# Small transfers of a decoder block issued by POOL and ScalarE instead of SyncE

## The chip, the cores and the metric

The kernel runs on one core of one Trainium2 chip, in one launch. The metric is the device time of one execution in microseconds (us). Four engines compute: TensorE (PE, with its weight loads shown apart as PEld), VectorE (DVE), ScalarE (ACT) and GpSimd (POOL). SyncE (SP) computes nothing here; it only issues transfers (DMAs). Every engine works through its own instructions strictly in order, and an instruction that waits for a semaphore holds up all that stands behind it on that engine. An engine that issues a DMA spends some time on the issue itself; the bytes are then moved by 16 DMA engines that all issuers share.

## What is computed

One post-norm decoder block on a sequence of 16 meta tokens and 1024 input rows of width 1024, in float32. A combined projection feeds two mixers that run side by side: a grouped state-space model (S5: 32 groups of 16 channels, 64 complex states each) and a chunkwise matrix LSTM with four heads. Their gated sum goes through an output projection, a layer norm and a feed-forward network of width 4096. Cut to what matters:

```python
h = _layer_norm(concat([meta, x]), ln0_g, ln0_b)                 # 1040 rows
p = h @ w_in + b_in          # columns: u_s5 | q | k | v | o | i | f | g_s5 | g_m
y_s5 = _s5_mixer(u_s5, ...)  # x_t = Abar x_{t-1} + Bbar u_t ; y_t = Re(C x_t) + D u_t, per group
z = gelu(y_s5) @ s5_w_glu
y_s5 = z[..., :D] * sigmoid(z[..., D:])
q, k = split(silu(causal_depthwise_conv(concat([q, k]))))        # width 4
hm = _mlstm_mixer(q, k, v, i, f)                                 # 4 heads, chunkwise, with a running maximum
y_m = (sigmoid(o) * head_norm(hm)) @ m_w_out
mix = sigmoid(g_s5) * y_s5 + sigmoid(g_m) * y_m
h = _layer_norm(ALPHA * h + mix @ w_o, ln1_g, ln1_b)
ff = square(relu(h @ w_up + b_up)) @ w_down
out = _layer_norm(ALPHA * h + ff, ln2_g, ln2_b)[16:]
```

## The kernel before

Every float32 matrix product is made of three passes of a cheaper float32 form: each operand is split into a high part (rounded, by ACT: `whi`, L212) and a low part (the rest, by DVE: `wlo`, L213), and `mm3` (L226 to L228) adds high x high, low x high and high x low into one PSUM tile. In the trace the three passes of a projection read `mm<-hT_hi,whi` (L226), `mm<-hT_lo,whi` (L227) and `mm<-hT_hi,wlo` (L228).

The projection is cut into jobs, one per 128 output columns (or per head for the values v), in the order of a string `ORDER` (`q0 q1 v0 q2 v1 q3 o1 o0 v2 ... u0 u1 v3 u2 g0 u3 g1 ...`); glu, gate and output jobs follow, then the feed-forward part. A job's raw weights (`wraw`) are loaded by SP, and split while the job before it runs. Between the matmuls of a job the kernel calls `pump`, which advances six lanes of side work, each a generator that yields an estimate of how long to wait until its next step: the mLSTM heads (`ml`), the convolution (`cv`), the constants of the state-space model (`s5c`), its batches (`s5`), its GELU (`s5g`), and a lane `ah` that scales rows kept for the residual and prepares weights of the feed-forward part. A scheduler then fixes one order of instructions for each engine, by its own estimates of what each costs; it inserts the semaphores too. Almost all working tiles are slots of one pool of 30 buffers (tag `s`), so a load into a slot waits for whoever used that slot last.

The lanes that the change touches, with the names that the traces and orders use:

- **mLSTM, per head:** `bvt` is a broadcast bias (L319). The gates write two small rows to device memory, `grow_dr` (L410) and `wrow_dr` (L413). `bcast_row` (L425, L427) reads a head's part of each back, broadcast over 128 partitions, into `gB` and `wiB`. DVE turns `gB` into a mask (L443); ACT takes its exponential (L446, L447) and scales the keys `kw` with it (L459). `hraw` is a head's raw output; DVE normalises it (L505), PE transposes it (`pt`, L512). `hm_dr` (L892) keeps the finished heads.
- **State space, four batches of 8 groups:** `s5_pre` loads constants (L582 to L588). For each batch the constants lane (`s5c`) builds the matrices `s5P`, `s5Rr`, `s5Ri` (L695 to L718) and, through PE's `s5k` (L739, L740, which need `s5Ri`), the kernel `s5Kt` (L744). Then 16 transfers (L757) spread `s5Kt` into the triangular matrix `s5Mx`. POOL writes the seeds of a table of rotations `s5T` (L763 to L766) and DVE doubles it eight times, six operations a time (L571 to L576, in `cmul`).
- **A batch itself** (`s5_batch`): 8 transfers (L785) gather the inputs `s5U` from `us_dr`, which the projection job u wrote (L545). PE makes `s5z` (L801) from `s5U`; ACT and DVE copy it out (L811, L809); DVE multiplies by the table (L816 to L819), adds (L821, L822), scans (L827), multiplies back (L837 to L840) and adds (L845). PE makes `s5y` from `s5Mx` and `s5U` (L856) and from the scan's result `s5w` (L857). The output goes out to `ys_dr` (L862), comes back rearranged in 8 transfers as `s5yc` (L870), and ACT takes the GELU (L873), which the glu jobs need.
- **Rows and prepared weights** (`ah_scale`, `up_early`): eight tiles of normalised rows are read (`ahr`, L1163), scaled and shifted by DVE and written back (`ah_dr`, L1174). Six weight tiles `wur` (L1190) become 21 prepared tiles that are stored (`wu_dr`, L1200) and read again much later as `wpre` (L1411).

All of these transfers stand on SP, among the weight loads; only the 21 loads `wpre` are issued by POOL.

Of the kernel before, what the change touches and what calls it, by code (L numbers as in the profile page):

```python
# [14 lines left out]
P = 128  # L15
# [97 lines left out]
def decoder_block(  # L113
# [24 lines left out]
    def f32(ap):  # L138
        return ap.bitcast(F32)
# [170 lines left out]
    def v_job(h):  # L310
# [6 lines left out]
        def run(job):  # L317
            bvt = mid.tile([P, DV], F32, tag="bvt", bufs=1, name="bvt")
            nc.sync.dma_start(bvt, row_bcast(bv, DV, h * DV))  # L319
            if h == 0:  # L320
# [43 lines left out]
    def gates():  # L364
        with ExitStack() as gc:
# [43 lines left out]
            v_.tensor_tensor_scan(gg, one, a, mp, op0=OP.add, op1=OP.max)  # L409
            nc.sync.dma_start(grow_dr, gg)  # L410
            wi = gt("lf2")
            a_.activation(wi, gg, AF.Exp, scale=-1.0, bias=mp)
            nc.sync.dma_start(wrow_dr, wi)  # L413
            em = gt("fr2")
# [9 lines left out]
    def bcast_row(dst, src, h):  # L424
        nc.sync.dma_start(dst[:, 0:META], bass.AP(tensor=src.tensor, offset=src.offset + h * P,  # L425
                                                  ap=[[0, P], [1, META]]))
        nc.sync.dma_start(dst[:, META:LEN].rearrange("p (c s) -> p c s", s=P),  # L427
                          bass.AP(tensor=src.tensor, offset=src.offset + (4 + h) * P,
                                  ap=[[0, P], [4 * P, NCH - 1], [1, P]]))
# [104 lines left out]
    def u_job(i):  # L534
        st = {}

        def evac(bi, c0, c1, ps):
            if bi == 0:
                st["u"] = slot("uT")
            o = st["u"][:, :LEN].rearrange("p (j c) -> p c j", j=8)  # L540
            a_.activation(o[:, c0 // 8:c1 // 8, :], ps.rearrange("p (c j) -> p c j", j=8), AF.Identity,
                          bias=bft[:, JU + i:JU + i + 1])

        def done():
            nc.sync.dma_start(us_dr[i * P:(i + 1) * P].rearrange("p j c -> p (j c)"), st["u"][:, :LEN])  # L545
            UD.add(i)
            lanes["s5c"].add(s5_consts(i))
            lanes["s5"].add(s5_batch(i))
        fm_job(JU + i, BLK, 0, evac, done)
# [28 lines left out]
    def s5_pre():  # L578
        def t16(name):
            return mid.tile([P, 16], F32, name="s5_" + name)  # L580
        lam = mid.tile([P, 112], F32, tag="row", bufs=1, name="s5_lam")[:, :48].rearrange("p (a b) -> p a b", a=3)
        nc.sync.dma_start(lam, s5l)  # L582
        bc = slot("s5bc")
        nc.sync.dma_start(bc[:, 0:512], s5b)
        nc.sync.dma_start(bc[:, 512:1024], s5c)
        S5["bc"] = bc
        dtl = mid.tile([32, 16], F32, name="s5_d")
        nc.sync.dma_start(dtl, s5d)  # L588
        S5["d"] = dtl
# [83 lines left out]
    def s5_consts(b):  # L673
# [81 lines left out]
        for j in range(8):  # L755
            for g2 in range(2):
                nc.sync.dma_start(mx[16 * j:16 * j + 16, :, g2, 16 * j:P],  # L757
                                  kt[16 * g2:16 * g2 + 16, :, 0:P - 16 * j])
# [21 lines left out]
    def u_load(b):  # L780
        U = slot("s5U")
        uv = U[:, :8 * NB].rearrange("p (g c) -> p g c", g=8)
        for j in range(8):
            src = us_dr[b * P:(b + 1) * P, j, :].rearrange("(g h) c -> h g c", h=16)
            nc.sync.dma_start(uv[16 * j:16 * j + 16], src)  # L785
        S5["u", b] = U
        return U

    def s5_batch(b):
# [60 lines left out]
        for hf in range(2):  # L850
# [10 lines left out]
            yield Y5[b]  # L861
        nc.sync.dma_start(ys_dr[b].rearrange("p g c -> p (g c)"), Y[:, 0:1024])  # L862
        lanes["s5g"].add(s5_gelu(b))

    def s5_gelu(b):
        yield 3.0
        yc = slot("s5yc")
        for g in range(8):
            src = ys_dr[b, :, (g % 2) * 4 + g // 2, :].rearrange("(t h) c -> h t c", h=16)
            nc.sync.dma_start(yc[16 * g:16 * g + 16, 0:1024].rearrange("p (t c) -> p t c", t=8), src)  # L870
        yield 14.0
# [12 lines left out]
    def o_job(f):  # L884
        def evac(bi, c0, c1, ps):
            if bi == 0:
                o_job.s = slot("osig")
            a_.activation(o_job.s[:, c0:c1], ps, AF.Sigmoid, bias=bft[:, JO + f:JO + f + 1])
            v_.tensor_tensor(HM[f][:, c0:c1], HM[f][:, c0:c1], o_job.s[:, c0:c1], op=OP.mult)

        def done():
            nc.sync.dma_start(hm_dr[f], HM.pop(f)[:, :D])  # L892
        fm_job(JO + f, HALF, META, evac, done)
# [261 lines left out]
    def ah_scale():  # L1155
        gb = [slot("gB0"), slot("bB0")]
        for i in range(2):
            nc.sync.dma_start(gb[i][:, :D], row_bcast(ln0r, D, i * D))
        rs = {}
        for t in range(9):  # L1160
            if t < 8:
                rs[t] = slot("ahr")
                nc.sync.dma_start(rs[t][:, :D], ah0_dr[t * P:(t + 1) * P, :])  # L1163
            if t == 0:
# [6 lines left out]
            for i, op in enumerate((OP.mult, OP.add)):  # L1171
                v_.tensor_tensor(r[:, :D], r[:, :D], gb[i][:, :D], op=op)
                yield 1.5
            nc.sync.dma_start(ah_dr[(t - 1) * P:t * P, :], r[:, :D])  # L1174

# [10 lines left out]
    def up_early():  # L1186
        for p in range(PRE):
            r = [slot("wur"), slot("wur")]
            for j in range(2):
                nc.sync.dma_start(r[j][:, :D], wup[2 * p + j].rearrange("p k f -> p (k f)"))  # L1190
            yield 3.0
# [3 lines left out]
            for n, w in ((1, a11), (2, a12), (3, n2[:, 0:512]), (4, a22), (5, n1[:, 0:512]), (6, n1[:, 512:1024]),  # L1195
# [3 lines left out]
                v_.tensor_tensor(o[:, 512:1024], w, f32(o[:, 0:512]), op=OP.subtract)  # L1199
                nc.sync.dma_start(wu_dr[p, n - 1], f32(o[:, 0:1024]))  # L1200
                yield 0.9
# [666 lines left out]
```

## Time and profile before

| | us |
|---|---|
| median of three executions | 1559.34 (1558.19 to 1671.65) |
| the profiled execution | 1557.0 |
| its span in the trace | 1555.2 |
| PE busy | 1525.8 (98%) |
| DVE busy | 1013.5 (65%) |
| ACT busy | 613.9 (39%) |
| POOL busy | 28.4 (2%) |

The span runs from the first to the last instruction that the trace holds; 1.8 us of the profiled execution lie around it. SP computes nothing and has no busy time on the page; its issues can be read in a timeline or by tile, where it is written SPq. In rows by line or tile, `x` is a number of instructions, and three numbers with slashes are the shortest, median and longest duration in ns. In a table of windows each engine has its busy time in that stretch, and `PEclk`, the third number from the end, is the clock granted to TensorE (1.00 is full speed). A row of waits reads: engine, tile and line that waited, `<-` what ended the wait, then us in total, times, and the longest.

### The profile page before, as it was taken

Reading aid. Unit: us, or ns where it says so; the run is one execution under the profiler, and the core shown is the slowest. Engines: PE = TensorE matmul, PEld = TensorE weight load, DVE = VectorE, ACT = ScalarE, POOL = GpSimd, SP = SyncE. Lnnn points to the kernel's source line nnn. Section 1 sums busy time; section 2 is a strip of 40 time slices with the busy share of each in tenths; the row PEclk is TensorE's granted clock in tenths of the full one; section 3 lists DMA queues with packets and bytes.
Section 4 is the critical chain, followed back from the end, with each engine's and each line's share of the span. In section 5 each row is a group of like instructions: output and inputs, shape, how many; then the busy total and the mean of one; then the engine's idle time right before and its main releaser. Section 6 shows DMA issues by size and latency. Waiting matters only on the chain.

```text
span 1555.2 us, 20386 instructions
## 1 busy us (share of the span) xinstructions
PE 1525.8 (98%) x7677; PEld 1287.7 (83%) x7677; DVE 1013.5 (65%) x2007; ACT 613.9 (39%) x950; POOL 28.4 (2%) x99
## 2 busy tenths in 40 slices
PE   8999999998999999999999999999999999999997
PEld 8999998997878778878888887888888888888886
DVE  7676565678668655742228576666666689766786
ACT  6533434335454333331115334444444534433340
POOL 0000000000000000000000001000000000000000
PEclk9999999999999999999999999999999999999999
DMA  6302113304222566731114328544443897767642
GB/s 249 111 19 79 63 42 99 96 22 114 84 77 65 160 245 228 266 140 41 55 59 174 107 79 263 199 149 149 150 149 122 274 390 269 241 220 240 217 170 103
DMA packets 105058, 232.53 MB, mean 150 GB/s; under 512 B 15912, under 2 KB 33776, under 8 KB 104960
## 3 DMA queue, kind: packets, MB, share of 16 engines
q1 hardware_dynamic: 101936, 220.22, 41.2%
q0 software_dynamic: 3024, 11.01, 2.2%
q8 instruction: 60, 0.98, 0.3%
q14 instruction: 38, 0.31, 0.1%
HBM read 164.41 MB, written 65.61 MB: 148 GB/s over the span
## 4 chain that ended last, share of the span: by engine, by line
PE 76%; issue 16%; DVE 3%; ACT 2%; DMA 2%; SPq 1%; POOLq 0%; DVEq 0%; ACTq 0%
PE mm L226 20%; PE mm L228 20%; PE mm L227 20%; PE sd L227 2%; PE sd L226 2%; PE sd L228 2%; PE mm L1091 2%; DMA wiB<-wrow_dr 1%; PE mm L1099 1%; PE pu L476 1%; PE pn L472 1%; PE pn L473 1%; SPq L757 1%; PE ln L1050 0%; PE s5z L801 0%
## 5 line engine op out<-in xcount | busy, mean ns | idle before, releaser
L226 PE MATMUL mm<-hT_hi,whi 128*128 128x512 f32 (+3 forms) x576 | 217.8, 378 | 1.4 <-ACT whi L212 1.4
L227 PE MATMUL mm<-hT_lo,whi 128*128 128x512 f32 (+3 forms) x576 | 215.6, 374 | 0.0
L228 PE MATMUL mm<-hT_hi,wlo 128*128 128x512 f32 (+3 forms) x576 | 214.9, 376 | 0.0
L213 DVE TENSOR_TENSOR wlo<-wraw,whi 128x1024 fp32r<-128x1024 f32 (+1 forms) x60 | 73.1, 1222 | 81.0 <-ACT whi L212 80.2
L226 PEld LDWEIGHTS mm<-hT_hi,whi 128*128 128x128 f32 x576 | 108.5, 188 | 18.1 <-ACT whi L212 1.8
L227 PEld LDWEIGHTS mm<-hT_lo,whi 128*128 128x128 f32 x576 | 108.5, 188 | 16.8 <-issue 0.4
L228 PEld LDWEIGHTS mm<-hT_hi,wlo 128*128 128x128 f32 x576 | 108.2, 188 | 16.6 <-issue 0.3
L212 ACT ACTIVATE whi<-wraw 128x1024 fp32r<-128x1024 f32 (+1 forms) x60 | 63.0, 1055 | 80.7 <-PE mm L227 74.1
L227 PE MATMUL sd<-dwl,dah 128*128 128x512 f32 x240 | 94.7, 394 | 0.0
L226 PE MATMUL sd<-dwh,dah 128*128 128x512 f32 x240 | 94.3, 393 | 0.0
L228 PE MATMUL sd<-dwh,dal 128*128 128x512 f32 x240 | 94.1, 393 | 0.0
L1563 ACT ACTIVATE dah<-da 128x1024 fp32r<-128x1024 f32 x56 | 58.6, 1051 | 88.5 <-PE sd L227 35.8
L1567 ACT ACTIVATE dwh<-wdr 128x1024 fp32r<-128x1024 f32 x56 | 58.9, 1054 | 81.4 <-DVE wdr L1549 23.7
L226 PE MATMUL mm<-dwh,dah 128*128 128x512 f32 (+1 forms) x224 | 84.7, 379 | 0.0
L227 PE MATMUL mm<-dwl,dah 128*128 128x512 f32 (+1 forms) x224 | 84.5, 378 | 0.0
L228 PE MATMUL mm<-dwh,dal 128*128 128x512 f32 (+1 forms) x224 | 84.4, 378 | 0.0
L1564 DVE TENSOR_TENSOR dal<-da,dah 128x1024 fp32r<-128x1024 f32 x56 | 68.1, 1219 | 19.0 <-ACT dah L1563 18.9
L1568 DVE TENSOR_TENSOR dwl<-wdr,dwh 128x1024 fp32r<-128x1024 f32 x56 | 68.2, 1219 | 11.0 <-ACT dwh L1567 10.5
L226 PE MATMUL mm<-whi,hT_hi 128*128 128x256 f32 (+1 forms) x256 | 74.5, 291 | 0.0
L228 PE MATMUL mm<-whi,hT_lo 128*128 128x256 f32 (+1 forms) x256 | 73.6, 288 | 0.0
L227 PE MATMUL mm<-wlo,hT_hi 128*128 128x256 f32 (+1 forms) x256 | 72.9, 285 | 0.0
L226 PE MATMUL mm<-th,wuh 128*128 128x512 f32 x156 | 61.7, 395 | 0.0
(443 smaller groups left out, 3590.9 us busy)
## 6 DMA issues: line engine op xcount, KB each, us to landing
da<-act_dr SPq DMA_DIRECT2D x56, 512.0 KB, 4.8
wdr<-in_wdn_dram SPq DMA_DIRECT2D x56, 512.0 KB, 5.7
wraw<-in_wf_dram SPq DMA_DIRECT2D x36, 512.0 KB, 4.9
wur<-in_wup_dram SPq DMA_DIRECT2D x32, 512.0 KB, 4.5
act_dr<-upy SPq DMA_DIRECT2D x64, 256.0 KB, 2.4
wu_dr<-wpre SPq DMA_DIRECT2D x21, 512.0 KB, 5.2
wpre<-wu_dr POOLq DMA_DIRECT2D x21, 512.0 KB, 4.6
act_dr<-upx SPq DMA_DIRECT2D x32, 256.0 KB, 4.0
```

The source lines that it names most:

```text
L212: a_.activation(hi[:, :n], r[:, :n], AF.Copy)
L213: todo.append(lambda e=v_, r=r, hi=hi, lo=lo, n=n: e.tensor_tensor(lo[:, :n], r[:, :n], f32(hi[:, :n]), op=OP.subtract))
L226: t_.matmul(ps, ah, bh, start=(i == 0 and part[0]), stop=False, skip_group_check=skip)
L227: t_.matmul(ps, ah, bl, start=False, stop=False, skip_group_check=skip)
L228: t_.matmul(ps, al, bh, start=False, stop=(i == n - 1 and part[1]), skip_group_check=skip)
L472: t_.matmul(pn[:, :257], qi[:, c0:c0 + n], Cs[c][:, :257], start=True, stop=False)
L473: t_.matmul(pn[:, :257], sws[c], vt[c][:, :257], start=False, stop=True)
L1091: t_.matmul(acc[w][:, :c1 - c0], jobs[i].w[0][a][:, k * P:(k + 1) * P], (hT_hi, hT_lo)[b][:, k, c0:c1], start=(first and k == 0), stop=(la ...
L1563: a_.activation(ah[:, :D], a[:, :D], AF.Copy)
L1564: v_.tensor_tensor(alo[:, :D], a[:, :D], f32(ah[:, :D]), op=OP.subtract)
L1567: a_.activation(wh, raw[i], AF.Copy)
L1568: v_.tensor_tensor(wl, raw[i], f32(wh), op=OP.subtract)
```

## The change

Twenty-odd calls `nc.sync.dma_start` become `g_.dma_start` (POOL) or `a_.dma_start` (ScalarE); what is transferred, and from where to where, stays as it is.

- To POOL: `bvt` 4, `grow_dr` 1, the broadcasts of `gB` and `wiB` 16, the state-space constants 4, `s5Mx` 64, `s5U` 32, `s5yc` 32, `hm_dr` 8, the scaled rows with their two broadcasts 18, `wur` 6 of 32, `wu_dr` 21: 206 transfers, beside the 21 that it had.
- To ScalarE: `wrow_dr` 1, `us_dr` 4, `ys_dr` 4.
- SP keeps the loads of weights and inputs and what the feed-forward part moves.

```diff
@@ run of v_job, gates, bcast_row
-            nc.sync.dma_start(bvt, row_bcast(bv, DV, h * DV))
+            g_.dma_start(bvt, row_bcast(bv, DV, h * DV))
...
-            nc.sync.dma_start(grow_dr, gg)
+            g_.dma_start(grow_dr, gg)
...
-            nc.sync.dma_start(wrow_dr, wi)
+            a_.dma_start(wrow_dr, wi)
...
-        nc.sync.dma_start(dst[:, 0:META], bass.AP(tensor=src.tensor, offset=src.offset + h * P,
+        g_.dma_start(dst[:, 0:META], bass.AP(tensor=src.tensor, offset=src.offset + h * P,
...
-        nc.sync.dma_start(dst[:, META:LEN].rearrange("p (c s) -> p c s", s=P),
+        g_.dma_start(dst[:, META:LEN].rearrange("p (c s) -> p c s", s=P),
@@ u_job, s5_pre (four loads), s5_consts, u_load
-            nc.sync.dma_start(us_dr[i * P:(i + 1) * P].rearrange("p j c -> p (j c)"), st["u"][:, :LEN])
+            a_.dma_start(us_dr[i * P:(i + 1) * P].rearrange("p j c -> p (j c)"), st["u"][:, :LEN])
...
-        nc.sync.dma_start(lam, s5l)
+        g_.dma_start(lam, s5l)
...
-                nc.sync.dma_start(mx[16 * j:16 * j + 16, :, g2, 16 * j:P],
+                g_.dma_start(mx[16 * j:16 * j + 16, :, g2, 16 * j:P],
                                   kt[16 * g2:16 * g2 + 16, :, 0:P - 16 * j])
...
-            nc.sync.dma_start(uv[16 * j:16 * j + 16], src)
+            g_.dma_start(uv[16 * j:16 * j + 16], src)
@@ s5_batch, s5_gelu, o_job
-        nc.sync.dma_start(ys_dr[b].rearrange("p g c -> p (g c)"), Y[:, 0:1024])
+        a_.dma_start(ys_dr[b].rearrange("p g c -> p (g c)"), Y[:, 0:1024])
...
-            nc.sync.dma_start(yc[16 * g:16 * g + 16, 0:1024].rearrange("p (t c) -> p t c", t=8), src)
+            g_.dma_start(yc[16 * g:16 * g + 16, 0:1024].rearrange("p (t c) -> p t c", t=8), src)
...
-            nc.sync.dma_start(hm_dr[f], HM.pop(f)[:, :D])
+            g_.dma_start(hm_dr[f], HM.pop(f)[:, :D])
@@ ah_scale, up_early
-            nc.sync.dma_start(gb[i][:, :D], row_bcast(ln0r, D, i * D))
+            g_.dma_start(gb[i][:, :D], row_bcast(ln0r, D, i * D))
...
-                nc.sync.dma_start(rs[t][:, :D], ah0_dr[t * P:(t + 1) * P, :])
+                g_.dma_start(rs[t][:, :D], ah0_dr[t * P:(t + 1) * P, :])
...
-            nc.sync.dma_start(ah_dr[(t - 1) * P:t * P, :], r[:, :D])
+            g_.dma_start(ah_dr[(t - 1) * P:t * P, :], r[:, :D])
...
-                nc.sync.dma_start(r[j][:, :D], wup[2 * p + j].rearrange("p k f -> p (k f)"))
+                g_.dma_start(r[j][:, :D], wup[2 * p + j].rearrange("p k f -> p (k f)"))
...
-                nc.sync.dma_start(wu_dr[p, n - 1], f32(o[:, 0:1024]))
+                g_.dma_start(wu_dr[p, n - 1], f32(o[:, 0:1024]))
```

The scheduler makes a new order of the whole mixer part from this. Three places matter below. In all rows a line number comes first, then the operation, what it writes and reads, the shape, and `x` with a count of equal neighbours.

**The last batch's transfers.** On SP before, the inputs `s5U` of batch 3 stand around the 16 transfers of its `s5Mx`:

```order
L785 DMA s5U<-us_dr 16x8x130 x3
L757 DMA s5Mx<-s5Kt 16x4x128 x2
L757 DMA s5Mx<-s5Kt 16x4x112 x2
L757 DMA s5Mx<-s5Kt 16x4x96 x2
L757 DMA s5Mx<-s5Kt 16x4x80 x2
L757 DMA s5Mx<-s5Kt 16x4x64 x2
L757 DMA s5Mx<-s5Kt 16x4x48 x2
L757 DMA s5Mx<-s5Kt 16x4x32 x2
L757 DMA s5Mx<-s5Kt 16x4x16 x2
L785 DMA s5U<-us_dr 16x8x130 x5
```

On POOL after, for the same batch (the `s5T` rows are the table's seeds):

```order
L785 DMA s5U<-us_dr 16x8x130 x8
L763 MEMSET s5T 128x4
L764 MEMSET s5T 128x4
L765 COPY s5T<-s_p_3045 128x4
L766 COPY s5T<-s_p_3045 128x4
L757 DMA s5Mx<-s5Kt 16x4x128 x2
L757 DMA s5Mx<-s5Kt 16x4x112 x2
L757 DMA s5Mx<-s5Kt 16x4x96 x2
L757 DMA s5Mx<-s5Kt 16x4x80 x2
```

All eight loads of `s5U` and the seeds now stand ahead of `s5Mx`.

**The table of batch 0.** On POOL before, the seeds of batch 0's table follow a memset:

```order
L722 MEMSET s5Rr 128x256
L335 MEMSET v_3350 128x1 x4
L752 MEMSET s5Mx 128x1024
L763 MEMSET s5T 128x4
L764 MEMSET s5T 128x4
L765 COPY s5T<-s_p_3045 128x4
L766 COPY s5T<-s_p_3045 128x4
```

On POOL after, the 16 transfers of `s5Mx` stand between them (the last six rows of eight kinds here):

```order
L757 DMA s5Mx<-s5Kt 16x4x96 x2
L757 DMA s5Mx<-s5Kt 16x4x80 x2
L757 DMA s5Mx<-s5Kt 16x4x64 x2
L757 DMA s5Mx<-s5Kt 16x4x48 x2
L757 DMA s5Mx<-s5Kt 16x4x32 x2
L757 DMA s5Mx<-s5Kt 16x4x16 x2
L763 MEMSET s5T 128x4
L764 MEMSET s5T 128x4
L765 COPY s5T<-s_p_3045 128x4
L766 COPY s5T<-s_p_3045 128x4
```

So the seeds of batch 0 come behind its transfers; in batches 1 to 3 they stand ahead of them. On DVE after, the table's first operation stands ahead of the last four evictions L353 of value job 3 (`v12_3351`), which free the PSUM tiles `mm`:

```order
L497 BN_AGGR hmv_3379<-hst_3757 128x2
L173 RECIPROCAL hny_3843<-hny_3843 128x4
L571 TENSOR_TENSOR s5tt_3521<-s5T_3520 128x4
L353 TENSOR_TENSOR v12_3351<-mm_3620,bvt_3347 128x256
L572 TENSOR_TENSOR s5tt_3521<-s5T_3520 128x4
L353 TENSOR_TENSOR v12_3351<-mm_3663,bvt_3347 128x256
```

Further on, DVE before, from the copies of the state-space input to the last constant that PE's `s5k` needs (`s5Z_3764` and `s5w_3871`, `s5w_3872` belong to batch 0, `s5Ri_3832` to the constants of batch 1; the table `s5T_3520` of batch 0 is long finished here):

```order
L505 TENSOR_SCALAR hraw_3378<-hraw_3378,hmv_3379,hny_3843 128x256 x4
L809 COPY s5Z_3764<-s5z_3850 64x130 x2
L816 TENSOR_TENSOR s5w_3871<-s5Z_3764,s5T_3520 128x520
L819 TENSOR_TENSOR s5w_3872<-s5Z_3764,s5T_3520 128x520
L817 TENSOR_TENSOR s5w_3872<-s5Z_3764,s5T_3520 128x520
L818 TENSOR_TENSOR s5w_3871<-s5Z_3764,s5T_3520 128x520
L718 SCALAR_TENSOR_TENSOR s5Ri_3832<-s5tm_3833,s5tm_3834 128x576
```

After, the end of the same stretch; 39 of the table's 48 operations stand between the first copy L809 of `s5z_3850` and the product L816, and one more behind it:

```order
L576 TENSOR_TENSOR s5T_3520<-s5tt_3521 128x4x64
L571 TENSOR_TENSOR s5tt_3521<-s5T_3520 128x4
L572 TENSOR_TENSOR s5tt_3521<-s5T_3520 128x4
L573 TENSOR_TENSOR s5T_3520<-s5tt_3521 128x4
L574 TENSOR_TENSOR s5tt_3521<-s5T_3520 128x4
L575 TENSOR_TENSOR s5tt_3521<-s5T_3520 128x4
L816 TENSOR_TENSOR s5w_3871<-s5Z_3764,s5T_3520 128x520
L818 TENSOR_TENSOR s5w_3871<-s5Z_3764,s5T_3520 128x520
L576 TENSOR_TENSOR s5T_3520<-s5tt_3521 128x4
L817 TENSOR_TENSOR s5w_3872<-s5Z_3764,s5T_3520 128x520
L819 TENSOR_TENSOR s5w_3872<-s5Z_3764,s5T_3520 128x520
L718 SCALAR_TENSOR_TENSOR s5Ri_3832<-s5tm_3833,s5tm_3834 128x576
```

The table of batch 0 has moved from ahead of the copies to behind them, ahead of the products, of L718, and of all that follows on DVE.

**PE behind that table.** Before, when a new job (`mm_4157`, `mm_4205`, `mm_4248`: three blocks of columns with the weights `whi_4010`, `wlo_4011`) begins beside batch 0's output:

```order
L457 MATMUL pk_4265<-ident_74,kT_1971 16x128
L226 MATMUL mm_4157<-hT_hi_88,whi_4010 128x256
L227 MATMUL mm_4157<-hT_lo_89,whi_4010 128x256
L226 MATMUL mm_4205<-hT_hi_88,whi_4010 128x384
L227 MATMUL mm_4205<-hT_lo_89,whi_4010 128x384
L226 MATMUL mm_4248<-hT_hi_88,whi_4010 128x400
L227 MATMUL mm_4248<-hT_lo_89,whi_4010 128x400
L857 MATMUL s5y_4074<-s5w_3871,s5RS_3427 128x128
L856 MATMUL s5y_4074<-s5U_3171,s5Mx_3470 128x128
```

After:

```order
L457 MATMUL pk_4265<-ident_74,kT_1971 16x128
L226 MATMUL mm_4157<-hT_hi_88,whi_4010 128x256
L227 MATMUL mm_4157<-hT_lo_89,whi_4010 128x256
L226 MATMUL mm_4205<-hT_hi_88,whi_4010 128x384
L227 MATMUL mm_4205<-hT_lo_89,whi_4010 128x384
L226 MATMUL mm_4248<-hT_hi_88,whi_4010 128x400
L227 MATMUL mm_4248<-hT_lo_89,whi_4010 128x400
L228 MATMUL mm_4157<-hT_hi_88,wlo_4011 128x256
L226 MATMUL mm_4157<-hT_hi_88,whi_4010 128x256
```

PE now needs the low part `wlo_4011` directly behind the same six passes. On DVE that split stands behind L816 to L840, the eight masks L443, L744 and two of the four L845 of batch 0; before, it stood behind all four L845, L744 and a small copy L449, and behind the same chain.

More of the change, by code (lines that the diff above doesn't have):

```diff
@@ L581, in s5_pre @@
         lam = mid.tile([P, 112], F32, tag="row", bufs=1, name="s5_lam")[:, :48].rearrange("p (a b) -> p a b", a=3)
-        nc.sync.dma_start(lam, s5l)
+        g_.dma_start(lam, s5l)
         bc = slot("s5bc")
-        nc.sync.dma_start(bc[:, 0:512], s5b)
-        nc.sync.dma_start(bc[:, 512:1024], s5c)
+        g_.dma_start(bc[:, 0:512], s5b)
+        g_.dma_start(bc[:, 512:1024], s5c)
         S5["bc"] = bc
         dtl = mid.tile([32, 16], F32, name="s5_d")
-        nc.sync.dma_start(dtl, s5d)
+        g_.dma_start(dtl, s5d)
         S5["d"] = dtl
```

## Prediction

> **What bounds the kernel now.** I read the page first, then windows of 100 us for the stages that the change touches, then what PE waits for there, and last the chain and the timeline at the two longest waits. The page:
>
> ```profile
> span 1555.2 us, 20386 instructions
> PE 1525.8 (98%) x7677; PEld 1287.7 (83%) x7677; DVE 1013.5 (65%) x2007; ACT 613.9 (39%) x950; POOL 28.4 (2%) x99
> ```
>
> PE sets the time. The moved lanes run from about 100 to 700 us; the windows there, and one later (PE busy is the first time after the comma):
>
> ```profile
> 100.00:200.00 100.00, 99.09 (x631) 92.95 (x631) 64.67 (x195) 45.62 (x66) 0.52 (x9) 1.00 0.21 63
> 200.00:300.00 100.00, 100.00 (x623) 91.11 (x622) 54.51 (x188) 39.36 (x66) 2.50 (x18) 1.00 0.25 81
> 300.00:400.00 100.00, 95.13 (x613) 87.42 (x612) 81.19 (x262) 39.14 (x78) 5.06 (x16) 0.98 0.27 74
> 400.00:500.00 100.00, 95.49 (x480) 77.48 (x479) 73.11 (x208) 49.04 (x76) 4.01 (x11) 1.00 0.25 74
> 500.00:600.00 100.00, 95.83 (x439) 78.36 (x438) 61.00 (x116) 37.21 (x50) 0.00 (x0) 0.98 0.57 196
> 600.00:700.00 100.00, 99.79 (x431) 80.61 (x431) 59.81 (x80) 36.08 (x50) 0.00 (x0) 1.00 0.57 210
> 700.00:800.00 100.00, 100.00 (x432) 80.83 (x432) 23.04 (x27) 15.30 (x18) 0.00 (x0) 1.00 0.11 37
> ```
>
> PE is idle for 0.91 + 0 + 4.87 + 4.51 + 4.17 + 0.21 = 14.7 us of these 600, at full clock. That is all the change can win in its stages: under 1% of the time. The last row gives the price of a full pass of 512 columns: 100 / 432 = 0.2315 us. What PE waits for from 100 to 700:
>
> ```profile
> PE s5y L857 <- DVE s5w L845: 5.2, 3, 3.6
> PE s5z L801 <- DMA s5U<-us_dr: 3.2, 1, 3.2
> PE pt L512 <- DVE hraw L505: 1.7, 1, 1.7
> PE mm L226 <- ACT whi L212: 1.6, 3, 1.2
> PE pu L476 <- ACT kw L459: 0.9, 1, 0.9
> ```
>
> Only one, 3.2 us, is a wait for a transfer that moves. The chain of waits ahead of it shows SP's queue: the 16 transfers L757 go out at 0.6 us apiece, and the last five loads of `s5U` behind them.
>
> ```profile
> 500.16 0.60 SPq L757
> ...
> 513.07 2.53 DMA s5U<-us_dr
> ```
>
> **The change part by part**, against the profiled execution of 1557.0 us (span 1555.2 and 1.8 around it), which is 2.3 under the median.
>
> *The price of an issue.* By tile, what POOL issues today, a row of SP's, and POOL's own copy of a seed beside a busy DVE:
>
> ```profile
> L1411 POOL DMA_DIRECT2D wpre<-wu_dr x21: 530/530/706, 806.5 to 970.3; - x21
> L757 SPq DMA_DIRECT2D s5Mx<-s5Kt x64: 585/593/1698, 323.4 to 510.9; - x64
> L765 POOL COPY s5T<-s_p x4: 193/455/1788, 319.0 to 488.2; 128x4 f32<-128x4 f32 x4
> ```
>
> I take 0.53 us for an issue on POOL: its shortest and its median, and less than the 0.593 that SP takes for L757; the upper bound is the copy's 1.79 (it was held). The `wpre` issues are the nearest row: transfers of 128 rows. All moved ones have no more pieces except L427, which has 8 pieces for each of 128 partitions. The 206 issues cost 109 us of a POOL that is 2% busy, so they are free unless another instruction waits in the queue behind them. On ScalarE nine issues at SP's 0.593 make 5 us of a unit that is 61% idle; I take nothing. From issue to landing, the same 512 KB:
>
> ```profile
> wur<-in_wup_dram SPq DMA_DIRECT2D x32, 512.0 KB, 4.5
> wpre<-wu_dr POOLq DMA_DIRECT2D x21, 512.0 KB, 4.6
> ```
>
> So a transfer from POOL lands 0.1 us later, and I take no more. The Trainium skill ("DMA: Bandwidth & Descriptors", section "Latency and other measured facts") gives the first byte at about 1 us by POOL's way and 0.6 by SP's; the rows above show a quarter of that difference. By the page, an estimate, three dependent transfers on the path (two for the first head, one for the last GELU) would add 1.2 us to the sum.
>
> *What goes: the wait for `s5U`.* On POOL all eight loads stand ahead of the seeds and of `s5Mx`, so they are issued some 10 us earlier relative to the 16 transfers: -3.2 us. What is late next there is DVE's L845 ahead of L857, as before.
>
> *What comes: batch 0's table on DVE.* The timeline of before at that place, DVE's rows, then PE's:
>
> ```profile
> 353.53 0.70 DVE L816 TENSOR_TENSOR s5w<-s5Z,s5T 128x520 f32<-128x520 f32 x1
> 355.98 0.75 DVE L718 SCALAR_TENSOR_TENSOR s5Ri<-s5tm 128x576 f32<-128x576 f32 x1
> 356.65 0.69 DVE L821 TENSOR_TENSOR s5Z<-s5w 128x520 f32<-128x520 f32 x1
> 357.87 2.67 DVE L827 TENSOR_TENSOR_SCAN s5w<-s_r,s5Z 128x130 f32<-128x130 f32 x8
> 360.57 0.67 DVE L837 TENSOR_TENSOR s5Z<-s5w,s5T 128x512 f32<-128x512 f32 x1
> 363.68 2.19 DVE L443 SCALAR_TENSOR_TENSOR gB<-gB,acol,mask 128x128 f32<-128x128 f32 x8 [0.63 <-DMA gB<-grow_dr]
> 368.39 2.11 DVE L845 TENSOR_TENSOR s5w<-s5Z,s5w 64x512 f32<-64x512 f32 x3
> 370.53 0.66 DVE L744 SCALAR_TENSOR_TENSOR s5Kt<-s_eye,s_d,s5Kt 32x16 f32<-32x16 f32 x4
> 371.12 1.21 DVE L213 TENSOR_TENSOR wlo<-wraw,whi 128x1024 fp32r<-128x1024 f32 x1
> ```
>
> ```profile
> 356.03 1.03 PE L512 MATMUL pt<-ident,hraw 128*128 128x128 f32 x8
> 360.36 0.60 PE L732 MATMUL s5p<-ident,s5P 128*128 128x128 f32 x4
> 362.44 0.38 PE L740 MATMUL s5k<-s5Ri,s5Rr 128*32 128x128 f32 x2
> 369.83 0.79 PE L857 MATMUL s5y<-s5w,s5RS 128*128 128x128 f32 x2 [3.64 <-DVE s5w L845]
> ```
>
> The table itself, one of its six groups from 100 to 600 us:
>
> ```profile
> L573 DVE TENSOR_TENSOR s5T<-s5tt 128x4 f32<-128x4 f32 (+6 forms) x32 | 7.2, 225 | 1.0
> ```
>
> Six groups of 7.0 to 7.2 us over four batches are 10.7 us a batch, of which 39 of 48 operations, the long ones among them, about 9.7 us, now stand between `s5z_3850` and L816.
>
> First wait, at the first L740: PE has 43 full passes (9.95 us), 16 transposes (1.03 + 2 x 0.60 = 2.2) and two short ones there, some 12.4 us. DVE has two copies (0.6), the table (9.7), four products (353.53 to 355.98: 2.45) and L718 (0.75): 13.5 us, after up to four L505 and two products for the constants that it may still be at, some 3 us by rows such as L816's. PE waits 1 to 4.5 us; I take 3, between the two.
>
> Second wait, at the first L228 of the new job. Behind L718, DVE has two additions (1.22), scans (2.58 until the next), the small mask (0.12), four products (2.41), eight masks (2.11), L744 (0.59), two L845 (1.40) and the split (1.21): 11.6 us. PE has the seven rest matmuls of `s5k` (0.22 each), a few short ones (0.3) and six passes of 256 to 400 columns (2 x 1040 columns at 0.2315 per 512: 0.94), 2.8 us. It waits 8.8. The waits of 1.2 (the longest for `whi`) and 3.64 us at this place go. Net: 3 + 8.8 - 4.8 = +7 us; between 0 (if the DVE stretch starts earlier than in before by the length of the table that it no longer does first) and +9.
>
> *The first head's broadcast.* L425 and L427 now follow `grow_dr` on POOL, and PE waits 0.9 us for `kw` already. If L427 costs by its pieces, eight times the 0.53 for each of two rows, it is up to +7; I take +2.
>
> *The last GELU.* On POOL the last eight `s5yc` stand behind the scaled rows of lane `ah`, whose stores wait for DVE. The glu jobs need them: 0 to +5, I take +2.
>
> *The rest of the new order*, 1133 lines on PE, among them weight loads on SP that now wait for POOL's transfers to free their slots: -3 to +5, I take +2, nearer to nothing than to the end since PE's waits outside the places above are 4 us in all.
>
> Sum: 7 - 3.2 + 2 + 2 + 2 = +9.8. 1557.0 + 10 = 1567 for the profiled execution, and with the 2.3 us to the median **1569**. The lower ends of the terms add up to -6, the upper ones to +23, so 1553 to 1582.
>
> **Rivals.** *POOL's issues are held.* In batch 0 the seeds stand behind 16 issues, which begin at 323.4; at d us each they are done at 323.4 + 16d + 0.9. DVE's first table operation stands ahead of four evictions L353 of a value job. In before the last of that job was at 332.7:
>
> ```profile
> 332.70 0.42 DVE L353 TENSOR_TENSOR v<-mm,bvt 128x256 f32<-128x256 f32 x1
> ```
>
> PE has one free tile more, 24 passes or 5.6 us, so it stands still when the seeds come after about 338. This decides from d = 0.85; at 0.53 they come at 332.8. If each issue is held as the copy L765 was (1.79 in all, or 0.53 and the 1.6 by which it exceeds its shortest: 2.13), the seeds come at 353 to 358 and PE loses 15 to 20 us. The last batch adds to it:
>
> ```profile
> L873 ACT ACTIVATE gelf<-s5yc x4: 2232/2303/2356, 418.1 to 569.8; 128x1024 f32<-128x1024 f32 x4
> s5yc<-ys_dr SPq DMA_DIRECT2D x32, 64.0 KB, 2.5
> ```
>
> From the first `s5Mx` of batch 3 (500.2) to the last GELU's start (569.8) less a landing of 2.5, POOL then has 41 transfers in 67 us, 1.64 each, so 6 to 20 us more. Together 21 to 40: 1590 to 1609, middle 1600. For it: L765, while DVE is 61 to 81% busy. Against: the 21 issues of L1411, at most 0.71 us beside this:
>
> ```profile
> 900.00:1000.00 100.00, 99.94 (x444) 80.83 (x443) 69.52 (x120) 42.57 (x76) 9.02 (x17) 1.00 0.60 197
> ```
>
> The Trainium skill ("SBUF — State Buffer", section "Who interferes with whom") has the mechanism: DVE's copies and scalar operations can lock POOL out while it writes descriptors; its figure is 3.1 us in place of 0.62 for a transfer. L1411 does not show it; if it holds, the time lies at this rival's upper end.
>
> *No slower.* The `s5U` wait goes, and DVE comes to the table early enough, because the work that stood behind it is done: then the place costs its old 4.8, and the broadcasts cost nothing. 1557 - 3.2 + 2 = 1556, and 1558 as a median; 1552 to 1561. For it: the change takes a wait out that is plainly there. Against: the second wait is counted from orders alone, and only a long PE queue could hide it.
>
> **How the numbers follow.** Forecast (1561 to 1582) 0.62; no slower 0.23; issues held 0.15, in part at first (1582 to 1590) and else in full. The range 1555 to 1592 leaves out the lower part of the second case and most of the third. A measurement of this kernel tells about 2% from no change, 31 us, so 1528 and 1590.5 are the bounds: faster 0.01, since all idle of these stages is half of that; slower 0.12, the held case without its beginning; same 0.87.
>
> **What would show it.** The rows of L757, L785 and L870 on POOL at 0.5 to 0.7 us; no wait of L801 for `s5U`; waits of PE at L740 for `s5Ri` and at L228 for `wlo`, together 8 to 13 us near 365; the windows 300:400 with PE busy near 90 and the others as before. The prediction is wrong if L757 on POOL is over 0.85 us with PE waiting for L353, if those two waits are missing, or if PE waits for weights behind SP.

## The result and the profile after

The changed kernel takes 1563.07 us (median of seven executions, 1562.08 to 1563.67) against 1558.78 for the kernel before: 1.0032 times as long, 95% interval 1.0022 to 1.0042. That is 4.3 us slower, where +10 was forecast: the right way and inside the range, but less than half of the size. One slow execution of the kernel before, 1671.65 us, is left out of the ratio. The two profiled executions differ by 6.7 us (spans 1561.9 and 1555.2); that is the difference that the lines below account for. The page of the changed kernel:

```profile
span 1561.9 us, 20418 instructions
PE 1527.0 (98%) x7677; PEld 1288.8 (83%) x7677; DVE 1012.7 (65%) x2007; ACT 616.9 (39%) x952; POOL 140.5 (9%) x305
```

POOL's 112 us more are issues, and they cost nothing by themselves: 206 more at about half a microsecond. By tile, the moved transfers, and POOL's copy of a seed:

```profile
L757 POOL DMA_DIRECT2D s5Mx<-s5Kt x64: 512/514/523, 323.6 to 518.2; - x64
L785 POOL DMA_DIRECT2D s5U<-us_dr x32: 528/531/564, 288.8 to 498.9; - x32
L870 POOL DMA_DIRECT2D s5yc<-ys_dr x32: 528/531/557, 391.0 to 570.5; - x32
L427 POOL DMA_DIRECT2D gB<-grow_dr x4: 902/914/988, 120.9 to 352.2; - x4
L765 POOL COPY s5T<-s_p x4: 203/386/3286, 331.8 to 499.4; 128x4 f32<-128x4 f32 x4
```

An issue of `s5Mx` is shorter on POOL (0.514 us) than on SP (0.593). The copy L765 was held up to 3.29 us beside DVE, but no issue was held: the longest of 64 took 0.523. Where PE is idle, by windows (first columns: PE's busy time):

```profile
100.00:200.00 100.00, 100.00 (x641) 93.99 (x640) 67.56 (x204) 45.90 (x66) 8.58 (x25) 1.00 0.23 59
300.00:400.00 100.00, 89.57 (x571) 82.53 (x571) 76.14 (x243) 37.24 (x70) 33.81 (x67) 0.93 0.26 69
500.00:600.00 100.00, 96.83 (x454) 78.39 (x453) 66.42 (x134) 36.61 (x49) 26.32 (x51) 0.98 0.52 172
```

PE's idle time from 300 to 400 us went from 4.9 to 10.4 us; from 500 to 600 it fell from 4.2 to 3.2. What PE waits for from 100 to 700 us now:

```profile
PE mm L228 <- DVE wlo L213: 6.7, 2, 5.2
PE s5k L740 <- DVE s5Ri L718: 2.8, 1, 2.8
PE pt L512 <- DVE hraw L505: 2.1, 1, 2.1
PE mm L226 <- ACT whi L212: 1.9, 4, 1.2
PE s5y L857 <- DVE s5w L845: 1.2, 1, 1.2
PE mm L226 <- DVE v L353: 0.9, 1, 0.9
```

The wait of 3.2 us for `s5U` and the one of 0.9 for `kw` are gone; the two forecast waits, for `s5Ri` at L740 and for `wlo` at L228, are there. The timeline shows the place: first POOL, then DVE, then PE.

```profile
323.61 8.11 POOL L757 DMA_DIRECT2D s5Mx<-s5Kt  x16 [14.72 <-DVE s5Kt L744]
331.77 0.20 POOL L765 COPY s5T<-s_p 128x4 f32<-128x4 f32 x1
```

```profile
340.35 0.13 DVE L571 TENSOR_TENSOR s5tt<-s5T 128x4 f32<-128x4 f32 x1
365.83 0.75 DVE L718 SCALAR_TENSOR_TENSOR s5Ri<-s5tm 128x576 f32<-128x576 f32 x1
376.94 1.22 DVE L213 TENSOR_TENSOR wlo<-wraw,whi 128x1024 fp32r<-128x1024 f32 x1
```

```profile
366.63 0.48 PE L740 MATMUL s5k<-s5Ri,s5Rr 128*32 128x128 f32 x2 [2.79 <-DVE s5Ri L718]
366.91 0.63 PE L739 MATMUL s5k<-s5Rr 128*32 128x128 f32 x2
371.81 0.38 PE L226 MATMUL mm<-hT_hi,whi 128*128 128x256 f32 x1 [1.19 <-ACT whi L212]
378.21 0.58 PE L228 MATMUL mm<-hT_hi,wlo 128*128 128x256 f32 x1 [5.19 <-DVE wlo L213]
```

The seeds of batch 0 are done at 332, eight microseconds before DVE comes to the table: no engine waits for them. The table is late because the order has it late.

To see where the 6.7 us lie, compare the times at which PE has done the same number of columns in both traces (worked out from the starts and shapes of its 7677 matmuls; the total is the same). By the times of the trace of before, the changed kernel loses 1.3 us by 20 us, gains 1.0 between 140 and 160, loses 2.5 from 300 to 360, 6.8 at 360 to 380, gains 0.9 by 420, gains 5.0 at 500 to 520 (and loses 0.8 around it), loses 2.6 from 580 to 600, and gains 1.0 spread over the rest. PE so ends 6.1 us later. The last 0.6 comes behind PE: from its last matmul to the end of the span it is 9.4 us against 8.8.

### The profile page after: what moved, and what is told of

The parts are those of the page before. It is cut to its first block, busy times and chain, and to the rows that moved or that the text cites. A ratio compares the mean times of both kernels' runs of the same rounds, so it can differ in the third digit from the quotient of the medians.

```text
span 1561.9 us, 20418 instructions
## 1 busy us (share of the span) xinstructions
PE 1527.0 (98%) x7677; PEld 1288.8 (83%) x7677; DVE 1012.7 (65%) x2007; ACT 616.9 (39%) x952; POOL 140.5 (9%) x305
## 4 chain that ended last, share of the span: by engine, by line
PE 77%; issue 16%; DVE 4%; ACT 1%; DMA 1%; POOL 0%; POOLq 0%; SPq 0%; DVEq 0%; ACTq 0%
PE mm L228 20%; PE mm L226 20%; PE mm L227 20%; PE sd L226 2%; PE sd L227 2%; PE sd L228 2%; PE mm L1091 2%; PE mm L1099 1%; PE pu L476 1%; PE pn L472 1%; PE pn L473 1%; DMA ahr<-ah_dr 1%; PE s5y L857 0%; PE ln L1050 0%; PE ln L1355 0%
## 5 line engine op out<-in xcount | busy, mean ns | idle before, releaser
L228 PE MATMUL mm<-hT_hi,wlo 128*128 128x512 f32 (+3 forms) x576 | 216.1, 377 | 5.2 <-DVE wlo L213 5.2
L228 PEld LDWEIGHTS mm<-hT_hi,wlo 128*128 128x128 f32 x576 | 109.2, 190 | 21.5 <-DVE wlo L213 5.5
L228 PE MATMUL sd<-dwh,dal 128*128 128x512 f32 x240 | 93.9, 392 | 0.0
L228 PE MATMUL mm<-dwh,dal 128*128 128x512 f32 (+1 forms) x224 | 84.3, 377 | 0.0
L228 PE MATMUL mm<-whi,hT_lo 128*128 128x256 f32 (+1 forms) x256 | 74.1, 289 | 0.0
```

Of the source, the lines that this page charges most:

```text
L228: t_.matmul(ps, al, bh, start=False, stop=(i == n - 1 and part[1]), skip_group_check=skip)
```

## The experiments

Theory A is that of the prediction: the new order costs, above all batch 0's table behind L757. Rival B: many small costs of issues and landings on POOL. Each kernel was timed beside the kernel before, and ratios are to it; where a time is set against the changed kernel's, that is its median of 1563.07.

### One lane moved alone: s5Mx on POOL

Edit, from the kernel before:

```diff
-                nc.sync.dma_start(mx[16 * j:16 * j + 16, :, g2, 16 * j:P],
+                g_.dma_start(mx[16 * j:16 * j + 16, :, g2, 16 * j:P],
```

> The kernel before with one lane moved: only the 64 transfers of s5Mx are issued by POOL. Theory A (the order: these 16 transfers stand on POOL ahead of batch 0's seeds, the scheduler puts the table late on DVE, and PE waits at L740 for s5Ri and at L228 for wlo): the two waits of 2.8 and 5.2 us of the change come back and the kernel is 5 to 8 us slower than before. Rival B (the loss is a sum of small things of all 206 transfers on POOL, issue times and later landings): a third of the transfers costs at most 2 us.

Measured: 1564.46 us against 1558.73, ratio 1.0040 (1.0028 to 1.0053), 5.7 us slower. A third of the transfers costs at least as much as the whole change. The two waits came back, in the waits of PE:

```profile
PE mm L228 <- DVE wlo L213: 4.0, 1, 4.0
PE s5k L740 <- DVE s5Ri L718: 2.9, 1, 2.9
```

That is what A forecast, but it isn't how the 5.7 come about. By equal PE work 8.2 us are lost from 320 to 380, and 5.4 are gained at 500 to 520: the wait for `s5U` is gone here too, since the 16 transfers that stood ahead of it on SP have left. So PE ends only 3.6 us later than in before, and 13.6 us pass from its last matmul to the end of the span, against 8.8. That was in no theory yet; it is taken up below.

### The changed kernel with the seeds first

The four POOL instructions L763 to L766 and their two slots are written ahead of the loop of transfers:

```diff
+        T = slot("s5T")
...
+        g_.tensor_copy(ts_[:, :, 1], S5["p8"][:, 1, q0:q0 + 4])
         Mx = slot("s5Mx")
```

> The changed kernel with one edit: the four POOL instructions that seed the table (L763 to L766) are written ahead of the 16 transfers of s5Mx. All transfers stay where the change put them. Theory A: the table returns to its early place on DVE, the waits at L740 and L228 go, and with the gain of the s5U loads kept the kernel is 6 to 10 us faster than the changed one, so 2 to 5 us faster than before. Rival B: nothing of the loss goes, within 2 us of the changed kernel.

Measured: 1553.06 us, ratio 0.9966 (0.9953 to 0.9979): 10.0 us faster than the changed kernel, with every transfer where the change put it. In the tile `s5T` of this run the table starts at 326.9 us, in the changed kernel at 340.4:

```profile
L571 DVE TENSOR_TENSOR s5tt<-s5T x32: 145/180/426, 326.9 to 509.0; 128x4 f32<-128x4 f32 x8, 128x8 f32<-128x8 f32 x4, 128x16 f32<-128x16 f32 x4, 128x32 f32<-128x32 f32 x4
```

and of PE's two waits one is gone and 1.8 us are left of the other:

```profile
PE s5y L857 <- DVE s5w L845: 4.0, 3, 2.2
PE mm L228 <- DVE wlo L213: 1.8, 2, 1.5
```

B falls. Moving four small instructions past 16 issues is worth more than the whole change. The edit also takes the slots of the table from the pool ahead of that of `s5Mx`; whether the new order of DVE comes from the one or from the other was not separated.

### The changed kernel with s5Mx back on SP

```diff
-                g_.dma_start(mx[16 * j:16 * j + 16, :, g2, 16 * j:P],
+                nc.sync.dma_start(mx[16 * j:16 * j + 16, :, g2, 16 * j:P],
```

> The changed kernel with s5Mx back on SP, all else on POOL and ScalarE. Theory A: the waits at L740 and L228 go here too, 5 to 9 us faster than the changed kernel. Rival B: a gain of some 2 us, by the share of the transfers.

Measured: 1561.36 us, ratio 1.0019 (1.0011 to 1.0028): only 1.7 us faster than the changed kernel, a miss for A's number. Its trace says why. The waits at L740 and L228 are gone (0.7 us left), and in the work that the kernel before has done by 380 us PE is 15 us ahead of the changed kernel, but in batch 1 the new order has another wait:

```profile
411.72 0.58 PE L857 MATMUL s5y<-s5w,s5RS 128*128 128x128 f32 x1 [5.83 <-DVE s5w L845]
```

PE still ends 8.4 us earlier than in the changed kernel, and then the stretch behind PE takes 15.2 us in place of 9.4.

### The broadcasts alone

From the kernel before, only `grow_dr`, `gB`, `wiB` to POOL and `wrow_dr` to ScalarE:

```diff
-            nc.sync.dma_start(grow_dr, gg)
+            g_.dma_start(grow_dr, gg)
...
-        nc.sync.dma_start(dst[:, 0:META], bass.AP(tensor=src.tensor, offset=src.offset + h * P,
+        g_.dma_start(dst[:, 0:META], bass.AP(tensor=src.tensor, offset=src.offset + h * P,
```

> The kernel before with only the gates' rows and their broadcasts moved (grow_dr and gB, wiB to POOL, wrow_dr to ScalarE). My prediction put the first head's broadcast at +2 us; the trace of the changed kernel has no wait of PE at all from 100 to 200 us, where before had 0.9 us. If the broadcast on POOL costs, 1 to 3 us slower than before; if it gains by leaving SP's queue, 1 to 3 us faster.

Measured: 1553.81 us, ratio 0.9976 (0.9964 to 0.9988), 4.9 us faster: more than either number. By equal PE work, 1 us of it comes at 140 to 160 us, where the first head's wait for `kw` is gone, and 4.8 at 360 to 380, where DVE's L845 of batch 0 no longer stand behind the masks L443 of the last head; 2.4 is given back at 400. DVE's timeline there:

```profile
361.77 0.67 DVE L845 TENSOR_TENSOR s5w<-s5Z,s5w 64x512 f32<-64x512 f32 x1
...
362.72 2.13 DVE L845 TENSOR_TENSOR s5w<-s5Z,s5w 64x512 f32<-64x512 f32 x3
364.88 1.93 DVE L443 SCALAR_TENSOR_TENSOR gB<-gB,acol,mask 128x128 f32<-128x128 f32 x7
```

So the term of my prediction that put this lane at +2 had the wrong sign; most of the gain lies at 360 to 380, in the new order of DVE.

### s5U alone

From the kernel before, only L785 on POOL.

> The kernel before with one lane moved: only the 32 loads of s5U are issued by POOL. By my prediction's term the last batch's wait of 3.2 us for s5U goes and nothing else changes: 3 us faster than before. If every lane that leaves SP makes the scheduler choose a new order of DVE and PE that gives and takes some us elsewhere (what the first runs point to), the s5U wait is gone in the trace all the same, but the time is anywhere from 3 us faster to 3 us slower.

Measured: 1558.27 us against 1557.08, ratio 1.0003 (0.9993 to 1.0012). The wait for `s5U` is gone from the trace, and the time is the same: the new order gains 5.3 us at 360 to 380 and loses 6.2 in batch 1, and 2.4 us more pass behind PE.

### The early loads back on SP

The changed kernel with `bvt` and the constants of the state space on SP again (L319, L582 to L588).

> The changed kernel with the loads of bvt and of the state-space constants (8 transfers, two of them issued by POOL in the first 3 us) back on SP. In the changed kernel's trace the first layer norm waits for its row block some 2.6 us longer than in the trace of before, and PE is 1.3 us behind at 20 us. If these early transfers of POOL cause it, the kernel is 1 to 2 us faster than the changed one; if it is the spread of single executions, there is no difference (within 1 us).

Measured: 1560.73 us, ratio 1.0025 (1.0015 to 1.0034), 2.3 us faster than the changed kernel by the medians, but only 1.1 by the two ratios, whose intervals overlap. Its PE is 1.1 us ahead of the changed kernel at 20 us and another 1.1 and 1.7 at 390 and 590. The first agrees with the early transfers as cause, but the first layer norm's wait differs by 1 us between other traces too, so this is not shown.

### The GELU's lane back on SP

```diff
-            g_.dma_start(yc[16 * g:16 * g + 16, 0:1024].rearrange("p (t c) -> p t c", t=8), src)
+            nc.sync.dma_start(yc[16 * g:16 * g + 16, 0:1024].rearrange("p (t c) -> p t c", t=8), src)
...
-        a_.dma_start(ys_dr[b].rearrange("p g c -> p (g c)"), Y[:, 0:1024])
+        nc.sync.dma_start(ys_dr[b].rearrange("p g c -> p (g c)"), Y[:, 0:1024])
```

> The changed kernel with the lane of the GELU's input (ys_dr and s5yc) back on SP. PE loses 2.6 us between 580 and 600 us in the changed kernel. If that comes from s5yc standing on POOL behind the scaled rows (my prediction's term of the last GELU, +2), it goes: 2 to 3 us faster than the changed kernel. If it comes from the rest of the new order, no difference.

Measured: 1571.94 us, ratio 1.0094 (1.0077 to 1.0110): 8.9 us slower than the changed kernel, against both expectations. On SP the GELU is late, not on POOL, as a wait of PE shows that the changed kernel doesn't have:

```profile
PE mm L226 <- ACT gelh L876: 2.4, 1, 2.4
```

So the 2.6 us that the changed kernel loses at 580 to 600 don't come back by moving this lane to SP. But this costs little: PE ends 1.2 us later than in the changed kernel. The other 7.3 come behind PE, 16.7 us in place of 9.4.

### Seeds first, GELU's lane and early loads on SP

> A combination that should beat both: the changed kernel with the seeds written ahead of the s5Mx transfers, and with the GELU lane and the early loads back on SP. If the three gains add up: 5.7 us under the time of before by the seeds, 2 to 3 more by the GELU lane and 1 by the early loads, so 9 us faster than before, some 1549.5. If the gains are only the luck of one order, no better than the seeds alone, 1553.

Measured: 1557.24 us, ratio 1.0000 (0.9991 to 1.0008). PE ends at 1539.6, half a microsecond before the seeds alone (1540.1), and 16.0 us pass behind it in place of 9.4. The gains did not add up, and the end took the rest.

### What stands behind PE: POOL's closing DRAIN

The last instructions of the kernel are the same everywhere; what differs is a DRAIN on POOL, for which the closing barrier of all engines waits. In eleven of the fourteen traces the stretch behind PE is the length of this DRAIN and 5.34 to 5.36 us; only in the kernel before, with `s5U` alone and in the last version is it 0.3 to 0.6 us more. Rows of the closing line by kernel, the longest of three is the one meant. Before:

```profile
L1864 POOLq DRAIN  x3: 40/102/2986, 1551.0 to 1555.0; - x3
```

`s5Mx` alone on POOL:

```profile
L1864 POOLq DRAIN  x3: 46/98/8217, 1554.6 to 1563.3; - x3
```

The GELU's lane on SP, the rest on POOL:

```profile
L1864 POOLq DRAIN  x3: 46/98/11317, 1558.2 to 1570.0; - x3
```

The changed kernel:

```profile
L1864 POOLq DRAIN  x3: 46/98/4052, 1557.0 to 1561.6; - x3
```

With 21, 38, 53 and 85 transfers on POOL it takes 2.99, 4.37, 5.60 and 8.22 us: each further transfer adds 0.082. To test this alone, 64 transfers that nothing waits for were added to the kernel before:

```diff
+        [g_.dma_start(idle_dr[i:i + 1, :], wu_dr[PRE - 1, 0, i:i + 1, 0:P]) for i in range(64)]
```

> The kernel before with 64 small transfers that nothing waits for (512 bytes each, from the prepared weights to a scratch row) added on POOL at a place where POOL is idle; every engine's order is otherwise the same. In the traces so far POOL's last instruction, a DRAIN behind its closing addition, takes 2.99 us in the kernel before (21 transfers on POOL), 4.37 with 38, 5.60 with 53 and 8.22 with 85: 0.082 us for each transfer. Theory C (the closing DRAIN pays for each transfer that POOL issued): PE ends as before, the DRAIN takes 8.2 us, the kernel is 4.5 to 5.5 us slower. Rival (the DRAIN's length comes from the lanes moved, their landings or their order): DRAIN 3 us and no difference in time.

Measured: 1564.11 us, ratio 1.0038 (1.0025 to 1.0052), 5.9 us slower, with the instructions of PE, DVE, ACT and SP in the same order:

```profile
L1864 POOLq DRAIN  x3: 40/93/8214, 1554.5 to 1563.2; - x3
```

The DRAIN is that of the other kernel with 85 transfers, to 3 ns, and 13.6 us pass behind PE. Theory C holds for this. One part of its expectation failed: PE did not end as before, but 3.5 us later than in the trace of before; 2.1 of that come at 140 to 160 us, where single executions differ (see below). The same with 206:

> The same with 206 small transfers, so 227 on POOL as in the changed kernel, whose DRAIN takes only 4.05 us. If the DRAIN pays for every transfer since the start, 0.082 x 206 + 3 = 19.8 us, and the kernel is 16 us slower. If transfers are written off in between by their number, the DRAIN takes about 4 us as in the changed kernel and the time is within 2 us of before. If they are written off by the pieces they hold (the changed kernel's have far more), it is nearer to 19.8.

Measured: 1565.54 us, ratio 1.0051 (1.0035 to 1.0067), DRAIN 9.93 us: neither 19.8 nor 4.05. By 0.082 apiece some 106 of 227 were still to be paid; in the changed kernel 34 of 227, with the GELU's lane on SP 123 of 195. So, if 0.082 is the price of each, some are written off on the way, and not by their number alone. What decides when is open.

### s5Mx on POOL, seeds first

The kernel before with `s5Mx` on POOL and the seeds ahead of it: the same 85 transfers as in the first run.

> The kernel before with the s5Mx transfers on POOL, as in the first run of that lane alone (5.7 us slower than before), but with the table's seeds written ahead of them. Both have 85 transfers on POOL, so the same closing DRAIN of 8.2 us; only the order differs. Theory A (the order costs): the waits at L740 and L228 go, 6 to 10 us faster than that run, so 0 to 4 us faster than before. Theory C alone (that run's loss was the DRAIN): no difference to that run, 5 us slower than before.

Measured: 1551.49 us, ratio 0.9964 (0.9952 to 0.9976): 13.0 us faster than that run by the medians and 11.8 by the ratios, with the same DRAIN (8.215 us). PE ends at 1535.9 in place of 1550.0. With lane, number of transfers and DRAIN equal, the place of four small instructions, with the order that the scheduler makes from it, decides over some 12 us. Here PE's waits for `s5U`, `s5Ri` and, but for 0.3 us, `wlo` are all gone.

### A version that beats both

Broadcasts on POOL, `us_dr` and `s5U` on ScalarE, `wpre` on SP; seeds, table and `s5Mx` as before. POOL issues 17 transfers.

```diff
-            nc.sync.dma_start(uv[16 * j:16 * j + 16], src)
+            a_.dma_start(uv[16 * j:16 * j + 16], src)
...
-        g_.dma_start(w, wu_dr[p, n - 1])
+        nc.sync.dma_start(f32(w), wu_dr[p, n - 1])
```

> A version meant to beat both: the kernel before with the gates' rows and broadcasts on POOL (and wrow_dr on ScalarE), the s5U loads and us_dr on ScalarE, and the 21 wpre loads on SP, so that POOL issues 17 transfers and its DRAIN is short. s5Mx, the seeds and the table stay as in before. If the s5U wait goes (3 us), the broadcasts gain as in their own run (4.9) and neither order nor DRAIN takes anything: 7 to 9 us faster than before, 1549 to 1551. If ScalarE's issues hold up its copies for PE, or the wpre loads are late on SP, at most 5 us faster.

Measured: 1546.22 us, ratio 0.9929 (0.9916 to 0.9942): 12.0 us faster than before, more than the 7 to 9 that were expected, and 17 faster than the changed kernel. By equal PE work 1.0 us is gained at 140 to 160, 4.9 at 360 to 380 and 5.0 at 500 to 520; the stretch behind PE is 8.6 us in place of 8.8. What each of the three edits gives here was not run apart. Its page and its closing DRAIN:

```profile
span 1544.4 us, 20362 instructions
PE 1522.0 (99%) x7677; PEld 1285.3 (83%) x7677; DVE 1013.3 (66%) x2007; ACT 615.5 (40%) x952; POOL 30.4 (2%) x95
```

```profile
L1864 POOLq DRAIN  x3: 40/98/2599, 1540.5 to 1544.2; - x3
```

## Why the prediction was right or wrong

- **What bounds it, and the price of an issue: right.** 0.53 us was taken; 0.51 to 0.53 came. L427 takes 0.91, far from the eightfold that bounded it. Landings are a little later on POOL, `s5yc` 2.8 us in place of 2.5. The Trainium skill ("DMA: Bandwidth & Descriptors", section "Latency and other measured facts") puts 0.4 us between the two ways; that is of this size, and no wait of PE shows it.
- **The wait for `s5U`: right, sized too small.** -3.2 was taken, 5.0 us were gained at that place. In before the granted clock in the window 500 to 520 was 0.91 and now it is 1.00: a wait of PE cost more than its length.
- **The two waits behind the table: the right place and cause, the size in part by luck.** +7 was forecast, as waits alone, and 6.8 came. But the waits at this place grew by only 4.3 us, from 4.8 (1.19 and 3.64) to 9.2 (2.79, 1.19 and 5.19); the other 2.4 came with matmuls behind them that ran slower. The first wait was 2.8 (3 taken). The second was 5.2, not 8.8, because PE needed longer for what lay between: pairs of `s5k` started 0.43 us apart where before they started 0.22 apart, and the wait of 1.2 for `whi`, which I had struck off, stayed. The sum came out since DVE's 11.6 us, from L718 at 366.5 to the end of the split at 378.1, set it.
- **The first head's broadcast: wrong, and the step that fails.** "I take +2" made a delay of PE out of a later landing, with DVE's order left as it was. It was -1.0 in the trace, 3.0 us less. The sum is too high by 3.1 us between the profiles; what the other terms miss nearly cancels (-1.8 and -0.2 above, +0.6, +0.7 and +0.6 below). The broadcast did come later: DVE's copy L449, which waits for `wiB`, starts at 133.11 where before it started at 131.06. But in before three operations L298 of the convolution stand on DVE between that copy and ACT's L301, and `kw` follows on ACT. After, only one does, so L301 and `kw` (140.82 in place of 142.64) come 1.7 and 1.8 us earlier. The last L298 is shown; before, then after:

```profile
131.06 0.17 DVE L449 COPY dec<-wiB 128x9 f32<-128x9 f32 x1 [1.68 <-DMA wiB<-wrow_dr]
135.26 1.28 DVE L298 SCALAR_TENSOR_TENSOR cy<-cpre,convt,cy 128x1040 f32<-128x1040 f32 x1
136.62 1.28 ACT L301 ACT_TABLE_LOAD   x1 [7.04 <-DVE cy L298]
```

```profile
133.11 0.17 DVE L449 COPY dec<-wiB 128x9 f32<-128x9 f32 x1 [1.83 <-DMA wiB<-wrow_dr]
133.54 1.29 DVE L298 SCALAR_TENSOR_TENSOR cy<-cpre,convt,cy 128x1040 f32<-128x1040 f32 x1
134.91 1.28 ACT L301 ACT_TABLE_LOAD   x1 [4.30 <-DVE s_ea L564]
```

- **The last GELU: near in size (+2 taken, 2.6 came), wrong in its cause.** Neither PE nor ACT has a wait for `s5yc` or the GELU in the changed kernel. At 580 to 600 PE waits for `wlo` (1.5 us) and for smaller things of the new order, and the granted clock there is 0.91 where before it was 1.00.
- **The rest of the order: +2 taken.** 1.3 at the start, 2.5 from 300 to 360, and about -1.1 elsewhere: 2.7 in sum. The 2.5 belong to batch 0's table as well: the run with the seeds first gains 2.5 there against the changed kernel.
- **The end: missing.** The closing DRAIN was in no term. In the changed kernel the stretch behind PE is only 0.6 us longer, by the luck of what had been written off: with 219 transfers on POOL (the early loads on SP) the DRAIN was 3.6 us, with 195 and 163 it was 11.3 and 9.8.
- **From the profile to the median: wrong by 3 us.** The terms as measured give 6.7 us between the profiled executions, not 9.8. I then added the 2.3 us by which the profile of before lay under its median. The changed kernel's profile lay 0.6 above its own. Executions of before lie between 1554.3 and 1561.0 us in the runs above, in part by the first head: in the run with 64 idle transfers, whose order is the same, L449 waits 2.56 us for `wiB` in place of 1.68, and PE falls 2.1 us behind before's trace between 140 and 160 us. Its wait there, and that window:

```profile
PE pu L476 <- ACT kw L459: 1.5, 1, 1.5
```

```profile
140.00:160.00 20.00, 18.52 (x128) 0.91 0.25 71
```

  The changed order has no such wait.
- **The rivals.** Issues held: out; in the rows of L757, L785 and L870 none took over 0.57 us. The Trainium skill ("SBUF — State Buffer", section "Who interferes with whom") has beside the lock that I quoted that additions and products of two tiles take only the port for reading, which writing descriptors is inferred not to need; that agrees: the copy L765 was held for 3.3 us and no issue was. No slower: not for this order, but the runs with the seeds first show that the moved transfers allow it.

## What to carry to other kernels

Where a scheduler sets the order, moving transfers to another queue is first of all a new order: look at what small instructions now stand behind a train of issues on the new issuer, and what the scheduler puts late because of them, before you price the issues. A transfer that lands later need not cost anything either, if the new order has put other work ahead of what waits for it, as at the first head. Write what a long chain depends on (here four seeds) ahead of the train. And read the end of the trace: with transfers on POOL the kernel's last barrier may wait for its DRAIN. Look at its length after each step, since the number of transfers alone does not tell it: it was 4.05 us with 227 and 11.3 with 195.

## What the runs showed of the hardware that was not expected

POOL's closing DRAIN grew by 0.082 us for each further transfer up to 85 (2.99 us with 21, 8.21 with 85), in three kernels with 85 the same to 3 ns; from 163 transfers on it was shorter than that, 4.05 us with 227 in the changed kernel and 9.93 with 227 of which 206 are small. And a wait of PE costs more than its length, as in these windows of 20 us, before and then after (the column behind PE's busy time is the granted clock):

```profile
360.00:380.00 20.00, 15.13 (x101) 0.91 0.45 106
```

```profile
360.00:380.00 20.00, 10.84 (x51) 0.76 0.38 98
```

PE was busy for 10.8 of 20 us there, at a granted clock of 0.76, and the waits' growth of 4.3 us became 6.8.
